# Branch weights in seven products, sums and lo parts on GpSimd, a wide third block: a change to a decoder layer on one core

## The chip, the core and the metric

The kernel runs on one core of one Trainium2 chip. The metric is the device time of one execution in microseconds (us). The names of the engines are those of the profile: PE is TensorE, DVE is VectorE, ACT is ScalarE, POOL is GpSimd, and SP is SyncE, which only issues DMAs here.

## The reference, cut to what matters

One decoder layer on x of 512 tokens by 1024, float32 throughout. Three token mixers are gated and added, then an output product, a feed-forward product with a gate, and two residuals:

```python
qa, ka, va, qb, kb, vb, qm, gl = split(rms_norm(x) @ w_in)
y_swa = swa_sink_attention(qa, ka, va, sinks, rel_bias)     # sliding window, 8 heads
y_sb  = stick_breaking_attention(qb, kb, vb)                # 8 heads
y_mem = memory_cross_attention(qm, mk, mv)                  # 4 heads, 256 memory rows
g = sigmoid(gl)                                             # 3 gates of 1024
merged = g[0] * (y_swa @ w_branch_swa) + g[1] * (y_sb @ w_branch_sb) + g[2] * (y_mem @ w_branch_mem)
h = x + rms_norm(merged @ w_out)
u = rms_norm(h)
out = h + rms_norm((silu(u @ w_gate) * (u @ w_up)) @ w_down)
```

Every product by y_ and w_branch_ is one of 512x512 by 512x1024. The weights w_gate and w_up have 2816 columns, 22 blocks of 128.

## The kernel before, in words

**Products in parts.** Each float32 operand is split in a hi part and a lo part (`split`, line 413: hi is rounded by ACT, lo = raw − hi is subtracted by DVE, from two SBUF operands). A product is hi·hi + hi·lo + lo·hi, three matmuls, each of 128 contracted rows and 256 or 512 columns.

**Seven products instead of eight.** Most of the large products are cut into two by two quarters and computed in the Strassen-Winograd way: seven products named p1 to p7 of sums of quarters, instead of eight. Sums of weight quarters are made by accumulating DMAs from POOL's queue, or by DVE; sums of the left operands by DVE. For the branch products, the ones in the list SEVENS (line 31) are made in sevens (`add_sevens`, `seven_*`), which are the sliding-window branch SWA and the memory branch MEM. The stick-breaking branch SB is made in eight by `add_branch`. `w_sum` (line 871) makes the weight sums of a branch in DRAM by two DMAs each on POOL's queue, started from unit SUM_FROM = 17 of the first half on. `seven_out` (line 907) multiplies a branch's result with its gate and adds the other branches; `gated` and `q_end` (lines 800 and 817) multiply the SB result with its gate as soon as the gate is there.

**Order of the first half.** After the projections come the heads (stick-breaking first), the three branches' gates, and the branch products. `sb_head` leaves z in three banks; ACT makes sigmoid(−z) and sigmoid(z) of it, POOL multiplies the blocks on the diagonal with the causal mask `seen` (lines 1272 to 1276: two operations of 128x128 and one of 128x2x128 for each head), DVE runs a scan along the keys, and PE transposes the result. Then come merging, w_out (loaded raw by `out_load`, split by `out_split`, line 1479), the norm, and the sums of the rows.

**Gate and up.** `gu` (line 1749) makes the block n (0 to 10) of w_gate and w_up together, in seven products for each n. A "banked" block (`banked`, line 1685) is wide: the moving operand holds the hi and the lo columns side by side, so hi·hi and hi·lo are one matmul of 512 columns, and only lo·hi is one of 256. Others take three matmuls of 256. Blocks 0 and 1 are narrow; from n = 3 on all are wide; in block 2 the banks y and w are wide and bank x, to which p1, p6, p7 and p4 go, is narrow. A wide block leaves two halves in PSUM, which `g_end` has to add: ACT copies one (t), then the other (t2, line 1711), and DVE adds them. `act_out` writes the activated quarters aq. After every second block `g_end` makes the sums of quarters sq, sr and aq(1,0) for the down product on DVE (line 1744).

**Down.** The products run in the order p1, p5, p6, p3, p7, p2, p4, each in six pieces c of up to 1024 weight columns (12 matmuls for the two halves of the tokens; `down`). For each piece ACT and DVE split the weights in hi and lo, in four buffers for each (hi0 to hi3, lo0 to lo3), and the left operands are split a few pieces ahead by `left_of` (line 1793) into lh and ll, tiles that rotate through a common ring. w_down arrives as raw for p1; p5 is made by an accumulating DMA of POOL's onto the same tile, after DVE has split p1's piece from it. p4 and p7 are made in the same way later, on POOL's queue. `dn_sum` adds two raw tiles on DVE for p6.

**What sets the order.** Each engine runs its instructions in its program's order. A table ORDER (from line 38 on) gives that order for each of the five engines by instruction numbers, and a table PLAN (from line 139 on) gives the place in the pools that each tile takes. Both are written out in the kernel. An instruction waits for its operands and for its tile's place, and all behind it on that engine wait with it.

Of the kernel before, what the change touches and what calls it, by code (L numbers as in the profile page):

```python
# [17 lines left out]
P = 128  # L18
# [12 lines left out]
SEVENS = (SWA, MEM,)  # L31
SUM_FROM = 17
# [25 lines left out]
    ),  # L58
    "vector": (
# [34 lines left out]
    ),  # L94
    "scalar": (
# [274 lines left out]
def tile_kernel(ctx, tc, a):  # L370
# [690 lines left out]
    for b in (SB, SWA, MEM):  # L1061
# [36 lines left out]
        if b in SEVENS:  # L1098
            add_sevens(b)
        elif b != SB:  # L1100
            add_branch(b)
# [1066 lines left out]
```

## Time and profile before

| What | us |
|---|---|
| median of 3 runs | 774.6 |
| lowest and highest | 774.45, 774.68 |
| the profiled execution | 774.24 |
| its span, first to last instruction | 772.4 |
| PE busy in it | 763.8 |
| DVE busy | 661.8 |
| ACT busy | 506.2 |
| POOL busy | 116.1 |

A row of the profile names the line of the instruction, its engine, its operation, what it writes and reads (out<-in), and its form. Every operation has line L222, since a helper records them, so tiles tell them apart: `bank` is PSUM, `lo<-raw,hi` the lo part of a weight tile, `bw` the stick-breaking weights of a head. In a timeline, the first column is the start and the second the duration, in us from the start of the span; neighbouring operations of one form are put together as xcount. An operation starts before its neighbour has ended where the engine overlaps them. A bracket gives the idle time ahead and what ended it.

### The profile page before, as it was taken

Reading aid. Unit: us, or ns where it says so; the run is one execution under the profiler, and the core shown is the slowest. Engines: PE = TensorE matmul, PEld = TensorE weight load, DVE = VectorE, ACT = ScalarE, POOL = GpSimd, SP = SyncE. Lnnn points to the kernel's source line nnn. Section 1 sums busy time; section 2 is a strip of 40 time slices with the busy share of each in tenths; the row PEclk is TensorE's granted clock in tenths of the full one; section 3 lists DMA queues with packets and bytes.
Section 4 is the critical chain, followed back from the end, with each engine's and each line's share of the span. In section 5 each row is a group of like instructions: output and inputs, shape, how many; then the busy total and the mean of one; then the engine's idle time right before and its main releaser. Section 6 shows DMA issues by size and latency. Waiting matters only on the chain.

```text
span 772.4 us, 11540 instructions
## 1 busy us (share of the span) xinstructions
PE 763.8 (99%) x4118; PEld 650.5 (84%) x4118; DVE 661.8 (86%) x1053; ACT 506.2 (66%) x916; POOL 116.1 (15%) x153
## 2 busy tenths in 40 slices
PE   9999999999999999999999999999999999999996
PEld 6889887778878888878888899988888888888885
DVE  7994797886796757999997589989999999999866
ACT  7662676796495758788935486566666668766552
POOL 3003363212002120011012001000000000214000
PEclk9999999999999999999999999999999999999999
DMA  8448998447239795579989338977777654959702
GB/s 304 145 132 245 340 253 251 138 130 157 56 82 189 194 195 185 136 188 247 390 200 294 101 93 238 251 209 181 205 192 207 179 157 150 204 136 242 168 1 109
DMA packets 48377, 144.28 MB, mean 187 GB/s; under 512 B 5760, under 2 KB 7344, under 8 KB 48256
## 3 DMA queue, kind: packets, MB, share of 16 engines
q1 hardware_dynamic: 33216, 92.55, 35.2%
q0 software_dynamic: 14672, 50.61, 33.6%
q8 instruction: 32, 0.52, 0.3%
q10 hardware_dynamic: 432, 0.39, 0.2%
q14 instruction: 25, 0.20, 0.1%
HBM read 134.61 MB, written 15.21 MB: 194 GB/s over the span
## 4 chain that ended last, share of the span: by engine, by line
PE 94%; DVE 2%; POOL 1%; ACT 1%; issue 1%; DVEq 0%; POOLq 0%; ACTq 0%
PE bank L222 94%; DVE bw L222 1%; POOL bw L222 0%; DVE lo L222 0%; POOL vnext L222 0%; POOL bias L222 0%; DVE wide L222 0%; ACT bw L222 0%; ACT L222 0%; ACT kas L222 0%; ACT br L222 0%; ACT hi L222 0%; DVE mks0l L222 0%; DVE fg L222 0%; ACT at L222 0%
## 5 line engine op out<-in xcount | busy, mean ns | idle before, releaser
L222 PE MATMUL bank<-pair,hi 128*128 128x512 f32 (+1 forms) x1064 | 263.2, 360 | 0.0
L222 PE MATMUL bank<-hi,pair 128*128 128x512 f32 (+1 forms) x696 | 215.8, 376 | 0.0
L222 PEld LDWEIGHTS bank<-pair,hi 128*128 128x128 f32 x1064 | 185.6, 189 | 26.6 <-issue 0.9
L222 DVE TENSOR_TENSOR lo<-raw,hi 128x1024 fp32r<-128x1024 f32 (+3 forms) x142 | 165.3, 1166 | 36.2 <-ACT hi L222 35.6
L222 ACT CAST hi<-raw 128x1024 fp32r<-128x1024 f32 (+3 forms) x142 | 143.3, 1012 | 79.2 <-PE bank L222 61.1
L222 PE MATMUL bank<-pair,lo 128*128 128x256 f32 (+1 forms) x776 | 166.3, 302 | 0.0
L222 PEld LDWEIGHTS bank<-hi,pair 128*128 128x128 f32 x696 | 128.1, 188 | 22.8 <-ACT mw L222 0.5
L222 PE MATMUL bank<-lo,pair 128*128 128x512 f32 (+1 forms) x362 | 136.0, 376 | 0.0
L222 PEld LDWEIGHTS bank<-pair,lo 128*128 128x128 f32 x776 | 122.0, 190 | 9.9
L222 ACT CAST hi<-wide 128x1024 fp32r<-128x1024 f32 (+1 forms) x62 | 63.2, 1024 | 35.9 <-PE bank L222 17.9
L222 PEld LDWEIGHTS bank<-lo,pair 128*128 128x128 f32 x362 | 68.0, 188 | 11.1
L222 DVE TENSOR_TENSOR lo<-wide,hi 128x1024 fp32r<-128x1024 f32 (+1 forms) x62 | 73.1, 1184 | 2.5 <-ACT hi L222 2.2
L222 POOL DMA_DIRECT2D raw<-in_w_g x24 | 21.0, 873 | 150.1 <-DVE lo L222 116.7
L222 DVE TENSOR_TENSOR gp<-gp,bank 128x512 f32<-128x512 f32 x48 | 32.9, 685 | 3.6 <-PE bank L222 2.7
L222 DVE TENSOR_TENSOR_SCAN bw<-br,bw 128x384 f32<-128x384 f32 (+3 forms) x32 | 29.1, 960 | 7.4 <-POOL bw L222 7.3
L222 POOL DMA_DIRECT2D raw<-in_w_gu x14 | 12.6, 943 | 128.8 <-DMA raw<-in_w_gu 128.6
L222 ACT ACTIVATE sg<-gp 128x256 f32<-128x256 f32 x41 | 17.3, 421 | 18.6 <-DVE gp L222 18.4
L222 POOL DMA_DIRECT2D wide<-in_w_gu x13 | 11.3, 873 | 106.4 <-DMA wide<-in_w_gu 90.8
L222 ACT COPY gp<-bank 128x512 f32<-128x512 f32 x41 | 23.9, 584 | 2.6 <-PE bank L222 2.6
L222 POOL TENSOR_TENSOR bw<-bw,wide 128x128 f32<-128x128 f32 (+1 forms) x24 | 18.6, 795 | 40.1 <-ACT bw L222 35.9
L222 DVE TENSOR_TENSOR gp<-gp,hp 128x512 f32<-128x512 f32 x33 | 22.5, 683 | 0.0
L222 DVE SCALAR_TENSOR_TENSOR s<-s,s 128x1 f32<-128x1 f32 x36 | 6.4, 177 | 17.6 <-ACT mt L222 10.5
(582 smaller groups left out, 1300.0 us busy)
## 6 DMA issues: line engine op xcount, KB each, us to landing
wide<-in_w_gu SPq DMA_DIRECT2D x30, 512.0 KB, 5.3
raw<-in_w_gu SPq DMA_DIRECT2D x27, 512.0 KB, 5.0
raw<-in_w_g POOLq DMA_DIRECT2D x24, 512.0 KB, 5.8
raw<-in_w_g SPq DMA_DIRECT2D x18, 512.0 KB, 3.8
raw<-in_w_p SPq DMA_DIRECT2D x14, 512.0 KB, 5.2
raw<-in_w_gu POOLq DMA_DIRECT2D x14, 512.0 KB, 7.6
wide<-in_w_gu POOLq DMA_DIRECT2D x13, 512.0 KB, 6.9
raw<-in_w_brt SPq DMA_DIRECT2D x10, 512.0 KB, 4.8
```

Source lines behind the costliest of these rows:

```text
L222: ins = f(*args, **kw)
```

## The change

- SB joins SEVENS: its branch product goes in seven quarter products, with `add_sevens(SB)` where `add_branch(SB)` stood. The weight sums start from unit 13 instead of 17, and there is one more branch of them: eight more DMAs on POOL's queue.
- The SB gate products (8 of 128x512) and the SWA adds in `seven_out` (8) go from DVE to POOL.
- The lo parts of w_out (16) go to POOL, and so do the lo parts of the left operands of the down product in pieces 0 to 4 (35), and the sums sq, sr and aq(1,0) of the column pairs 0 to 4 (15).
- The third mask operation of a stick-breaking head becomes two of 128x128.
- Bank x of gate and up block 2 is wide as well.
- ORDER and PLAN are drawn anew for all engines.

```diff
-SEVENS = (SWA, MEM,)
-SUM_FROM = 17
+SEVENS = (SB, SWA, MEM)
+SUM_FROM = 13
...
 ORDER = {
...
-        "1-2 0 98 3-15 20 17 16 18 21-23 19 24-27 41 28 42 29 43 30-32 47 44 38 35 33-34 45 48 53 49-52 46 36 54 59 55 "
+        "1-2 98 0 3-15 20 17 16 18 21-23 19 24-27 41 28 42 29 43 30-32 47 44 38 35 33-34 45 48 53 49-52 46 36 54 59 55 "
...
-    def split(raw, hi, lo):
+    def split(raw, hi, lo, eng=None):
...
-        lows = nc.vector.tensor_tensor(lo, raw, hi.bitcast(F32), op=ALU.subtract)
+        lows = (eng or nc.vector).tensor_tensor(lo, raw, hi.bitcast(F32), op=ALU.subtract)
...
-    def parts(name, t):
+    def parts(name, t, eng=None):
         h, l = ck(f"{name}h", F32R), ck(f"{name}l", F32R)
-        split(t[:, :], h[:, :], l[:, :])
+        split(t[:, :], h[:, :], l[:, :], eng)
...
             acc = acc_t[(t, h)]
-            nc.vector.tensor_tensor(acc[:, :], acc[:, :], x[:, :], op=ALU.mult)
+            nc.gpsimd.tensor_tensor(acc[:, :], acc[:, :], x[:, :], op=ALU.mult)
...
                 acc = acc_t[(2 + i, 0)]
-                nc.vector.tensor_tensor(acc[:, :], acc[:, :], t[:, :], op=ALU.mult)
+                nc.gpsimd.tensor_tensor(acc[:, :], acc[:, :], t[:, :], op=ALU.mult)
...
-        nc.vector.tensor_tensor(g[:, :], g[:, :], more[:, :], op=ALU.add)
+        (nc.gpsimd if b == SWA else nc.vector).tensor_tensor(g[:, :], g[:, :], more[:, :], op=ALU.add)
...
-    add_branch(SB)
+    add_sevens(SB)
...
-        if b in SEVENS:
+        if b != SB:
             add_sevens(b)
-        elif b != SB:
-            add_branch(b)
...
-            if i < 2:
-                nc.gpsimd.tensor_tensor(w[i][:, :P], w[i][:, :P], seen[:, :], op=ALU.mult)
-            else:
-                x = w[i][:, :].rearrange("p (b n) -> p b n", b=4)[:, 0:4:2, :]
-                nc.gpsimd.tensor_tensor(x, x, seen[:, :].unsqueeze(1).to_broadcast([P, 2, P]), op=ALU.mult)
+            for o in (0,) if i < 2 else (0, 256):
+                x = w[i][:, o : o + P]
+                nc.gpsimd.tensor_tensor(x, x, seen[:, :], op=ALU.mult)
...
-            wo[(h, k)] = parts(f"wo{h}{k}", t)
+            wo[(h, k)] = parts(f"wo{h}{k}", t, nc.gpsimd)
...
-        return n >= 2 and (n, b) != (2, "x")
+        return n >= 2
...
-            sub(sq[c], aq[(1, 0)][c], aq[(1, 1)][c], w)
-            sub(aq[(1, 0)][c], aq[(0, 0)][c], aq[(1, 0)][c], w)
+            eng = nc.gpsimd if n < HF - 1 else None
+            sub(sq[c], aq[(1, 0)][c], aq[(1, 1)][c], w, eng=eng)
+            sub(aq[(1, 0)][c], aq[(0, 0)][c], aq[(1, 0)][c], w, eng=eng)
             if n < HF - 1:
-                sub(sr[c], sq[c], aq[(0, 0)][c], w)
+                sub(sr[c], sq[c], aq[(0, 0)][c], w, eng=eng)
...
-    def sub(out, x, y, n, op=ALU.subtract):
-        nc.vector.tensor_tensor(out[:, :n], x[:, :n], y[:, :n], op=op)
+    def sub(out, x, y, n, op=ALU.subtract, eng=None):
+        (eng or nc.vector).tensor_tensor(out[:, :n], x[:, :n], y[:, :n], op=op)
...
-        split(x[:, :n], h[:, :n], l[:, :n])
+        split(x[:, :n], h[:, :n], l[:, :n], nc.gpsimd if c < NCH - 1 else None)
```

On POOL, at the start of the down phase, the rows before are DMAs alone. Those to `raw` and `wide` from in_w_dn accumulate into weight tiles of p5 (the first six rows) and of p4:

```order
L222 DMA raw_73<-in_w_dn 128x1024
L222 DMA wide_84<-in_w_dn 128x1024 x3
L222 DMA raw_74<-in_w_dn 128x1024
L222 DMA wide_84<-in_w_dn 128x512
L222 DMA raw_73<-in_w_dn 128x1024
L222 DMA wide_84<-in_w_dn 128x1024 x3
L222 DMA raw_74<-in_w_dn 128x1024
```

In the changed program the last DMAs of p5 stand in the same place, and operations of 128x512 between and behind them. Here `pair` and `ll` are lo tiles of the left operands, in the ring, and sq, sr and aq are sums of quarters:

```order
L230 DMA raw_73<-in_w_dn 128x1024
L230 TENSOR_TENSOR sq_5338<-aq_5084,aq_5110 128x512
L230 TENSOR_TENSOR aq_5084<-aq_5134,aq_5084 128x512
L230 DMA raw_75<-in_w_dn 128x1024
L230 DMA wide_84<-in_w_dn 128x512
L230 TENSOR_TENSOR ll_6338<-sq_5338,pair_109 128x512
L230 TENSOR_TENSOR sq_6047<-aq_5794,aq_5820 128x512
L230 TENSOR_TENSOR aq_5794<-aq_5844,aq_5794 128x512
L230 TENSOR_TENSOR pair_115<-aq_5084,pair_113 128x512
```

After the row of pair_115 fifteen more operations of 128x512 follow without a DMA between them, and then p4's first DMA. From p5's first DMA, which waits for DVE's split of p1's first piece, to p7's first one on a whole raw tile of p3 (it waits for the split of p3's first piece) there are 25 such operations.

On DVE, just behind the split of p1's second piece (`lo_81<-wide_84,hi_78`), the rows before hold lo parts of the left operands (`pair<-sq,lh`, `pair<-sq,pair`) between the splits of weights:

```order
L222 TENSOR_TENSOR lo_82<-wide_84,hi_76 128x1024
L222 TENSOR_TENSOR aq_6163<-gp_6032,sg_6161 128x256
L222 TENSOR_TENSOR pair_116<-sq_4944,lh_6279 128x512
L222 TENSOR_TENSOR pair_118<-aq_6163,pair_106 128x256
L222 TENSOR_TENSOR pair_111<-sq_5299,pair_115 128x512
L222 TENSOR_TENSOR pair_107<-sq_5654,pair_113 128x512
L222 TENSOR_TENSOR lo_83<-raw_74,hi_79 128x1024
```

In the changed program the splits there have the last column pair's work of 128x256 between them:

```order
L230 TENSOR_TENSOR lo_82<-raw_73,hi_76 128x1024
L230 TENSOR_TENSOR aq_6201<-gp_6071,sg_6199 128x256
L230 TENSOR_TENSOR gp_6225<-gp_6225,hp_6227 128x512
L230 TENSOR_TENSOR ll_6394<-sq_6234,pair_116 128x256
L230 TENSOR_TENSOR pair_106<-aq_6201,pair_111 128x256
L230 TENSOR_TENSOR sr_6341<-sq_6234,aq_6201 128x256
L230 TENSOR_TENSOR aq_6147<-aq_6201,aq_6147 128x256
L230 TENSOR_TENSOR lo_83<-raw_75,hi_79 128x1024
```

The three rows of 128x512 from sq are on POOL now. On PE, in gate and up block 2, the products of bank x took three matmuls of 256 columns for each k (two by hi, one by lo):

```order
L222 MATMUL bank_104<-pair_114,hi_78 128x256 x2
L222 MATMUL bank_104<-pair_114,lo_81 128x256
L222 MATMUL bank_104<-pair_106,hi_78 128x256 x2
L222 MATMUL bank_104<-pair_106,lo_81 128x256
L222 MATMUL bank_104<-pair_107,hi_77 128x512 x2
```

In the changed program they take one of 512 and one of 256:

```order
L230 MATMUL bank_104<-pair_111,hi_78 128x512 x2
L230 MATMUL bank_104<-pair_114,hi_78 128x512 x2
L230 MATMUL bank_104<-pair_111,lo_81 128x256 x2
L230 MATMUL bank_104<-pair_114,lo_81 128x256 x2
```

Over the program there are 64 matmuls of 256 columns fewer for that, and 32 of 512 more; the stick-breaking product has 12 of 512 fewer.

More of the change, by code (lines that the diff above doesn't have):

```diff
@@ L96 @@
         "0-16 21-22 18 17 19 23-25 20 26-29 38-39 30 40 31 43 32-33 41-42 34-35 46 36 44-45 37 49 47-48 52 50-51 55 53 "
[28 rows of a table removed]
[28 rows of a table added]
     ),
     "gpsimd": (
-        "4-11 15 31-32 3 0-1 13 12 14 2 39 41 53 55 40 42 54 56 16 21 46 26 29 28 30 60 33-35 20 18-19 17 22 24 23 "
-        "36-37 27 25 47 61 38 43-45 48 62 50-52 49 63 57-59 64-71 73 79 76 72 78 75 74 77 80-106 109 108 107 110-134 "
-        "143-148 139 135-138 140-142"
[8 rows of a table added]
     ),
     "sync": (
[5 rows of a table removed]
[5 rows of a table added]
     ),
@@ L140 @@
     "raw": (
-        "3 2 1 0 3 2 1 0 3 2 1 0 3 2 1 0 3 2 1 0 3 2 1 0 3 2 1 0 3 2 1 0 3 2 1 0 3 2 1 2 1 2 1 0 3 0 3 0 3 2 0 1 3 2 0 "
-        "1 3 2 3 2 3 2 0 3 1 2 0"
+        "0 1 2 3 0 1 2 3 0 1 2 3 0 1 2 3 0 1 2 3 0 1 2 3 0 1 2 3 0 1 2 3 0 1 2 3 0 1 2 3 0 1 0 1 0 1 2 3 2 3 2 3 0 1 2 "
+        "3 0 1 2 3 0 3 0 3 0 1 2 3 0 1"
     ),
     "hi": (
-        "3 2 1 0 3 2 1 0 3 2 1 0 3 2 1 0 3 2 1 0 3 2 1 0 3 2 1 0 3 2 1 0 3 2 1 0 2 3 1 0 2 3 1 0 2 3 1 0 2 3 1 0 2 3 1 "
-        "0 2 3 1 0 2 3 1 0 2 3 1 0 2 3 1 0 2 3 1 0 2 3 1 0 2 3 1 0 2 3 1 0 2 3 1"
+        "0 1 2 3 0 1 2 3 0 1 2 3 0 1 2 3 0 1 2 3 0 1 2 3 0 1 2 3 0 1 2 3 0 1 2 3 0 1 2 3 0 1 2 3 0 1 2 3 0 1 2 3 0 1 2 "
+        "3 0 1 2 3 0 1 2 3 0 1 2 3 0 1 2 3 0 1 2 3 0 1 2 3 0 1 2 3 0 1 2 3 0 1 2 3 0 1"
     ),
     "lo": (
-        "3 2 1 0 3 1 2 0 3 1 2 0 3 1 2 0 3 1 2 0 3 1 2 0 3 1 2 0 3 1 2 0 3 1 0 2 1 3 0 2 1 3 0 2 1 3 0 2 1 3 0 2 1 3 0 "
-        "2 1 3 0 2 1 3 0 2 1 3 0 2 1 3 0 2 1 3 0 2 1 3 0 2 1 3 0 2 1 3 0 2 1 3 0"
+        "0 1 2 3 0 1 2 3 0 1 2 3 0 1 2 3 0 1 2 3 0 1 2 3 0 1 2 3 0 1 2 3 0 1 2 3 0 1 2 3 0 1 2 3 0 1 2 3 0 1 2 3 0 1 2 "
+        "3 0 1 2 3 0 1 2 3 0 1 2 3 0 1 2 3 0 1 2 3 0 1 2 3 0 1 2 3 0 1 2 3 0 1 2 3 0 1"
     ),
     "p": (
[4 rows of a table removed]
[4 rows of a table added]
     ),
     "p2": (
-        "3 1 0 3 2 3 1 2 1 3 0 2 1 3 0 1 1 3 0 0 2 1 1 0 3 3"
+        "1 2 3 2 0 1 0 1 1 2 3 0 1 3 3 3 0 0 1 2 2 0 2 2 3 0 1"
     ),
     "ck": (
[19 rows of a table removed]
[20 rows of a table added]
     ),
     "ck2": (
-        "13 10 2 0 7 8 11 12 3 4 9 1 5 6"
+        "13 8 2 11 12 7 0 10 3 5 6 9 1 4"
     ),
@@ L193 @@
     "fraw": (
-        "8 1 3 2 0 7 6 5 4 8 1 3 2 0 7 8 4 5 2 6 3 7 1 0 8 5 6 4 2 3 1 8 0 7 5 4 3 2 6 1 0 5 7 8 4 2 1 3 6 0 7 4 8 5 2 "
-        "3 0 1 6 7 8 2 5 4 3 0"
+        "8 2 3 0 1 6 7 4 5 8 2 3 0 1 6 8 5 4 0 3 7 6 2 1 8 4 3 0 5 7 2 8 6 1 4 0 7 3 5 2 6 4 8 1 0 3 2 7 5 6 8 0 1 4 3 "
+        "7 6 5 2 8 1 3 4 0 7 6"
     ),
```

223 rows, old and new, of tables (ORDER, PLAN) are left out of this document.

## Prediction

> **What bounds the kernel now.** I read the page first: the busy shares, the slices, and the chain that ended last.
>
> ```profile
> PE 763.8 (99%) x4118; PEld 650.5 (84%) x4118; DVE 661.8 (86%) x1053; ACT 506.2 (66%) x916; POOL 116.1 (15%) x153
> PE   9999999999999999999999999999999999999996
> DVE  7994797886796757999997589989999999999866
> PE 94%; DVE 2%; POOL 1%; ACT 1%; issue 1%; DVEq 0%; POOLq 0%; ACTq 0%
> ```
>
> TensorE (PE) is busy in 99% of the span, in every slice but the last, and 94% of the last chain is its own. VectorE (DVE) stands at 9 in long runs of slices; GpSimd (POOL) is nearly empty. So time can be won only by taking matmul work away, and it is lost wherever another engine hands PE its operands late. How close the others are, the table of busy time by stage tells (window; length; PE; PEld; DVE; ACT; POOL; clock; DMA share; GB/s):
>
> ```profile
> 330.00:395.00 65.00, 65.00 (x300) 53.25 (x299) 64.61 (x96) 54.12 (x89) 6.99 (x8) 1.00 0.95 275
> 395.00:460.00 65.00, 65.00 (x376) 57.05 (x375) 49.73 (x106) 32.92 (x88) 6.48 (x8) 1.00 0.60 163
> 650.00:700.00 50.00, 50.00 (x236) 41.93 (x236) 49.63 (x71) 38.71 (x62) 10.79 (x13) 1.00 0.79 190
> 700.00:740.00 40.00, 40.00 (x178) 33.14 (x177) 35.49 (x58) 25.18 (x46) 6.76 (x8) 1.00 0.73 168
> ```
>
> PE is full in all of them, and DVE is full beside it in 330 to 395 (memory branch) and in 650 to 700 (the start of the down projection). The granted clock is 1.00 and plays no part. There DVE is the second bound, and there a change that makes DVE slower will show.
>
> **PE's gain.** PE's pace is the distance of neighbouring starts; the second column is longer because matmuls overlap.
>
> ```profile
> 439.65 0.39 PE L222 MATMUL bank<-wo15l,mgh 128*128 128x512 f32 x1
> 439.88 0.39 PE L222 MATMUL bank<-pair,mgl 128*128 128x512 f32 x1
> 440.11 0.39 PE L222 MATMUL bank<-wo16h,mgh 128*128 128x512 f32 x1
> 300.03 0.28 PE L222 MATMUL bank<-pair,qms0h 128*128 128x256 f32 x1
> 300.26 0.28 PE L222 MATMUL bank<-pair,pair 128*128 128x256 f32 x1
> ```
>
> A matmul of 512 columns takes 0.23 us (0.2275 over longer stretches), one of 256 takes (300.26 − 300.03) / 2, or 0.12. The stick-breaking branch product goes from eight quarter products to seven: 96 matmuls of 512 columns become 84, so 12 × 0.2275 = 2.73 us. In the third gate and up block, bank x goes wide: 96 matmuls of 256 become 32 of 512 and 32 of 256, so 64 × 0.12 − 32 × 0.2275 = 0.40. Together **−3.13 us**, all on the path, since PE is the path. That is all there is to win, beside the few waits that PE has.
>
> **What the move to GpSimd costs DVE.** By the program 82 two-input operations of 128x512 go onto POOL, most of them from DVE, which is relieved by about 37 us in all. The price is read where both engines already work at once: POOL's masks for the stick-breaking weights, and DVE's scans beside them (start; duration).
>
> ```profile
> 85.63 0.96 DVE L222 TENSOR_TENSOR_SCAN bw<-br,bw 128x384 f32<-128x384 f32 x1 [1.95 <-POOL bw L222]
> 86.81 0.73 POOL L222 TENSOR_TENSOR bw<-bw,wide 128x256 f32<-128x256 f32 x1
> 95.29 1.65 POOL L222 TENSOR_TENSOR bw<-bw,wide 128x256 f32<-128x256 f32 x1
> 96.33 1.42 DVE L222 TENSOR_TENSOR_SCAN bw<-br,bw 128x384 f32<-128x384 f32 x1
> 116.17 1.42 DVE L222 TENSOR_TENSOR_SCAN bw<-br,bw 128x384 f32<-128x384 f32 x1
> 85.14 0.46 POOL L222 TENSOR_TENSOR bw<-bw,wide 128x128 f32<-128x128 f32 x1 [0.66 <-ACT bw L222]
> 113.89 0.95 DVE L222 TENSOR_TENSOR mks0l<-mk,pair 128x512 fp32r<-128x512 f32 x1
> 94.36 0.69 DVE L222 SCALAR_TENSOR_TENSOR qa<-bank,wide 128x512 f32<-128x512 f32 x1 [0.80 <-PE bank L222]
> ```
>
> A scan of 128x384 takes 0.96 us when its POOL partner is small or done, and 1.42 when a 128x256 one is in its way: DVE lost 0.46 to 0.50 against an operation of 0.73. The POOL operation itself went from 0.73 to 1.65, that is by the length of a scan. So the two don't share, they take turns. Against a 128x128 one (0.46 alone) DVE's mks0l took 0.95, where other operations of its size take 0.68: 0.27 lost. Only DVE operations with both inputs in SBUF pay; qa, which reads a PSUM bank, kept its 0.69 with a POOL mask beside it.
>
> From 0.27 at 128 elements and 0.50 at 256 the line goes on to 0.50 + 2 × 0.23, about **0.95 us lost by DVE per POOL operation of 512** (an estimate from these rows; no operation of that size stands on POOL before). In the same way POOL's own time goes from 0.46 and 0.73 to about 1.28 alone, and to 1.28 plus one DVE operation when DVE is full. What DVE saves per moved operation is its pace (starts of neighbours):
>
> ```profile
> 654.23 1.22 DVE L222 TENSOR_TENSOR lo<-raw,hi 128x1024 fp32r<-128x1024 f32 x1
> 655.37 0.68 DVE L222 TENSOR_TENSOR pair<-aq,pair 128x512 fp32r<-128x512 f32 x1
> 655.97 1.40 DVE L222 TENSOR_TENSOR gp<-gp,bank 128x512 f32<-128x512 f32 x2
> 660.75 0.42 DVE L222 TENSOR_TENSOR aq<-gp,sg 128x256 f32<-128x256 f32 x1
> 661.09 0.68 DVE L222 TENSOR_TENSOR pair<-sq,lh 128x512 fp32r<-128x512 f32 x1
> ```
>
> 1.14 us for 1024 elements, 0.60 for 512, 0.34 for 256. So 0.60 is freed and up to 0.95 comes back as waiting: where DVE has time to spare this costs nothing, where it is full each move is a loss.
>
> The Trainium skill, "SBUF — State Buffer", section "Who interferes with whom", says that a DVE instruction with two SBUF inputs contends with a GpSimd one that reads SBUF, and that the loser blocks for the whole instruction. The turns in the rows agree with it; the size doesn't quite, for DVE lost 0.50 of 0.73, two thirds. With the whole 1.28 as the price, the sum below would end 7.6 us higher.
>
> **The down phase.** The program order puts a dense run of POOL work between the raw split of p1's first piece and that of p3's first, the stretch in which DVE was full before. These two splits, and PE's first matmuls on them:
>
> ```profile
> 701.08 1.22 DVE L222 TENSOR_TENSOR lo<-wide,hi 128x1024 fp32r<-128x1024 f32 x1
> 661.22 0.40 PE L222 MATMUL bank<-lo,pair 128*128 128x512 f32 x1
> 706.12 0.39 PE L222 MATMUL bank<-lo,pair 128*128 128x512 f32 x1
> 666.63 0.69 DVE L222 TENSOR_TENSOR lo<-wide,hi 128x512 fp32r<-128x512 f32 x1
> 674.84 0.39 PE L222 MATMUL bank<-lo,pair 128*128 128x512 f32 x1
> ```
>
> PE takes 706.12 − 661.22 = 44.9 us from one to the other. The first split was done at 655.45, 5.8 ahead of PE; the second at 702.30, 3.8 ahead. The greatest lead here was 7.5 (split done at 667.32, used at 674.84); the four lo buffers, freed by PE one unit of 2.73 us after the other, don't allow more than about 8. By the program DVE has 65 instructions between the two splits before (18 of 1024, 36 of 512, 11 of 256: 20.5 + 21.6 + 3.7 = 45.8 us, and the trace has 46.9) and 50 after (18, 19, 13: **36.2 us**). POOL has 25 operations of 128x512 in between, among DMA issues that wait for just these splits. Five of DVE's 50 read PSUM, 8% of its time, so 23 of the 25 are charged: 23 × 0.95 = 21.9, and DVE needs 58.1. It has 44.9 plus the lead it enters with. I give it 7.5, the greatest of before, since it is relieved ahead of the stretch too: 52.4, so PE waits 5.7; with the 5.8 of before it would wait 7.4. I take **+5.6 us** (0 to 7.4). The waits fall on the splits of p6 and p3, and what PE loses there never comes back.
>
> **The memory branch.** Sixteen lo parts of w_out and eight gated adds of the sliding-window branch go to POOL around 340 to 400. The lo parts are wanted later, and DVE has 65 − 49.7 = 15.3 us free in 395 to 460, so I let them cost nothing. The adds lie in the full stretch: 8 × (0.95 − 0.60) = 2.8 at most, and some of DVE's work beside them evacuates PSUM: **+1.5 us** (0 to 2.8).
>
> **Edits at nothing.** POOL also gets eight gate products of the stick-breaking heads and the masks in pieces of 128 (16 × 0.27 = 4.3 us of DVE's time for 8 × 0.50 = 4.0). They lie in 75 to 170, where DVE has 18 us free; at most 8 × 0.35 or 2.8, if each hits a scan that PE waits for.
>
> ```profile
> 75.00:170.00 95.00, 94.21 (x552) 77.50 (x551) 77.18 (x118) 69.76 (x141) 34.68 (x47) 1.00 0.78 230
> L222 POOL DMA_DIRECT2D raw<-in_w_g x24 | 21.0, 873 | 150.1 <-DVE lo L222 116.7 <-DVE s L222 32.7 <-DVE wide L222 0.7
> ```
>
> The sums of the stick-breaking weights add eight DMAs to POOL's queue at 0.87 us each, some between the masks of the heads, where a mask may come late; POOL was busy 34.7 of 95 there, so nothing. ACT's added copies, about 13 us, lie in its idle third.
>
> **The sum.** 774.24 (the profiled execution; its span is 772.4, 1.8 lies around it) − 3.1 + 5.6 + 1.5 = 778.2. The median of the runs shown, 774.6, is 0.36 above the profiled one: **778.6 us**. A measurement of this kernel can tell about 0.2%, 1.5 us, from no change.
>
> **Rivals.**
>
> *Faster: the price isn't paid on the path.* Then PE's 3.1 us remain: 771.5, or up to 773 with some waits. For it: what moved is wanted late, DVE is relieved of 37 us, and the price is stretched from operations a quarter and half as long. The point from which it decides: with a price of p per operation PE waits 36.2 + 23p − 52.4; that is zero below p = 0.70, and eats all 3.1 us at p = 0.84. The 0.95 isn't far above either, so 0.36.
>
> *No change:* p near 0.84, or a lead that is spent elsewhere: 773.1 to 776.1, with 0.11.
>
> *Slower by POOL's queue instead of DVE.* p4's and p7's accumulating DMAs stand behind the same run of operations on POOL, and the last pieces of p7 had no slack in before:
>
> ```profile
> 687.88 0.89 POOL L222 DMA_DIRECT2D raw<-in_w_dn  x1 [18.75 <-DVE lo L222]
> 702.59 0.88 POOL L222 DMA_DIRECT2D wide<-in_w_dn  x1 [2.00 <-DVE lo L222]
> 725.18 1.22 DVE L222 TENSOR_TENSOR lo<-raw,hi 128x1024 fp32r<-128x1024 f32 x1
> 726.75 0.39 PE L222 MATMUL bank<-lo,pair 128*128 128x512 f32 x1
> ```
>
> PE used that lo part 0.35 us after it was there. If DVE wins the turns, POOL takes 1.28 + 0.60 for each of the 25, 47 us, and 7 issues of 0.87 make it 53: about 3 more than the 50 at hand between these two splits. p7 then comes 3 to 6 us late, and the time is 774.6 − 3.1 + 3 to 6, 774.5 to 777.5. Against it: the order has p7's first DMAs ahead of p4's last, which takes some of that back. It has 0.08, half of it within 0.2%.
>
> **Chances and range.** Slower 0.49 (0.45 by DVE's price, 0.04 by POOL's queue), same 0.15 (0.11 and 0.04), faster 0.36. The likeliest case has 776.2 to 784.5 for itself: the top is 774.6 − 3.1 + 7.4 + 2.8 + 2.8. Since the cases of the other side hold half, the range goes down to 771.0: 771.5, less half a microsecond of waits that a new order may take away.
>
> **What would show it.** In the trace after: PE's work smaller by 3.1; POOL rows of 128x512 of 1.3 us alone and near 1.9 beside DVE; DVE splits of 128x1024, 1.22 before, at 1.8 to 2.2 in many places of the down phase; PE's waits named DVE lo, at p6 and p3. Splits that keep 1.22 while POOL works beside them would make the price wrong. Long splits without a wait of PE would make the lead wrong. A wait on DMA ahead of p7 would be the third case.

## The result and the profile after

| What | before | after |
|---|---|---|
| median, us | 774.5 | 813.6 (4 runs, 813.2 to 817.2) |
| ratio after to before | | 1.0515, interval 1.0485 to 1.0545 |
| the profiled execution | 774.24 | 817.21 |
| its span | 772.4 | 815.4 |

The changed kernel is 39 us slower, and 43.0 in the profiled pair: the profiled execution is the slowest of the four, so what the trace shows is 3.6 us more than the median has. The side was right, the size was not: 778.6 was forecast, 784.5 at most.

From the page of after, the busy shares, PE's slices, the granted clock, and the last chain:

```profile
PE 780.3 (96%) x4074; PEld 654.8 (80%) x4074; DVE 697.9 (86%) x988; ACT 516.2 (63%) x941; POOL 268.6 (33%) x251
PE   9999999999999999989899999999999998869796
PEclk9999999999999999999999999999999998979898
PE 50%; DVE 17%; issue 5%; ACT 4%; DMA 1%; DVEq 0%; ACTq 0%
```

DVE has 65 instructions fewer and is busy 36 us longer; POOL's busy time has more than doubled. PE has fewer matmuls and a longer busy time, with a granted clock below full in the last slices. The chain that was 94% PE's is half PE's now. The table of busy time by stage, same columns as before:

```profile
330.00:395.00 65.00, 61.85 (x275) 50.01 (x273) 54.19 (x65) 48.85 (x78) 32.68 (x22) 0.97 0.74 197
395.00:460.00 65.00, 62.06 (x308) 51.76 (x309) 48.02 (x94) 28.96 (x78) 19.53 (x17) 0.97 0.77 208
650.00:700.00 50.00, 44.24 (x215) 37.14 (x214) 49.45 (x48) 35.88 (x60) 29.86 (x22) 0.93 0.62 137
700.00:740.00 40.00, 32.00 (x117) 24.51 (x117) 38.42 (x26) 16.12 (x24) 33.66 (x21) 0.87 0.26 59
```

In the last row DVE is busy for 38.4 of 40 us with 26 instructions, where it did 58 before. PE's waits follow (sum, times, longest). Of the tiles, `gp` and `sy` are those in which DVE adds up the banks of a product, and `mpts20l` is the lo part of an operand of the memory branch:

```profile
PE bank L230 <- DVE lo L230: 12.5, 7, 4.8
PE bank L230 <- DVE gp L230: 5.1, 2, 4.2
PE bank L230 <- DVE sy L230: 3.0, 1, 3.0
PE bank L230 <- DVE mpts20l L230: 2.3, 1, 2.3
PE bank L230 <- DVE wide L230: 2.0, 3, 1.3
PE bank L230 <- ACT hi L230: 1.9, 1, 1.9
```

**Where the time went.** For every matmul I take the distance to the next start, less the pace of its size (0.227 us for 512 columns, 0.12 for 256). The paces add up to 757.2 us before and 754.0 after: the saved work is there, 3.2. What lies above them, in us by stage:

| Stage | 0–170 | 170–300 | 300–340 | 340–460 | 460–650 | 650–700 | 700–end | sum |
|---|---|---|---|---|---|---|---|---|
| before | 4.4 | 0.1 | 0.9 | 0.6 | 1.1 | 0.0 | −0.2 | 7.0 |
| after | 4.4 | 3.4 | 1.8 | 10.4 | 3.2 | 9.2 | 20.9 | 53.3 |

46.3 more, less 3.2, is 43.1; the spans differ by 43.0. Of the 46.3, 31.6 are waits of over 0.18 us, and 11.7 are matmuls at half pace (95 of them, 31 before), which the prediction had no term for. They stand behind the longer waits. PE in the changed kernel, behind its wait for `gp`, and the same group of work before that wait:

```profile
669.11 2.00 PE L230 MATMUL bank<-pair,hi 128*128 128x512 f32 x8
...
676.22 3.78 PE L230 MATMUL bank<-pair,hi 128*128 128x512 f32 x8 [4.16 <-DVE gp L230]
679.80 1.90 PE L230 MATMUL bank<-pair,lo 128*128 128x256 f32 x8
```

Eight matmuls take 3.78 us instead of 2.00, and the eight of 256 columns behind them 1.90, where they took 1.11 at 670.95. So the wait of 4.2 us costs some 2.6 us more. In this kernel a single wait of 2.35 us is enough:

```profile
349.48 0.50 PE L230 MATMUL bank<-mpts20l,pair 128*128 128x512 f32 x1 [2.35 <-DVE mpts20l L230]
...
350.96 0.63 PE L230 MATMUL bank<-hi,xsp50h 128*128 128x512 f32 x1
351.38 0.63 PE L230 MATMUL bank<-lo,xsp50h 128*128 128x512 f32 x1
```

From 350.96 the starts are 0.42 apart. Behind a wait of 1.16 us (at 698.08) they stay 0.23 apart. No single length divides the two cases: in all_back (below) eight such matmuls stand behind a wait of 1.82 us at 395.75, and in sums_back none behind one of 3.41 at 755.20.

**What DVE and POOL do to each other.** Both engines' timelines of the changed kernel at 700 us, DVE's rows and then POOL's:

```profile
702.41 2.31 DVE L230 TENSOR_TENSOR lo<-wide,hi 128x1024 fp32r<-128x1024 f32 x1
704.64 4.55 DVE L230 TENSOR_TENSOR lo<-raw,hi 128x1024 fp32r<-128x1024 f32 x2
```

```profile
701.37 2.27 POOL L230 TENSOR_TENSOR sr<-sq,aq 128x512 f32<-128x512 f32 x1
703.60 2.28 POOL L230 TENSOR_TENSOR pair<-aq,pair 128x512 fp32r<-128x512 f32 x1
705.83 2.28 POOL L230 TENSOR_TENSOR ll<-sr,lh 128x512 fp32r<-128x512 f32 x1
```

They take turns, one for one: a split starts every 2.23 us, where its pace was 1.14, so each POOL operation costs DVE 1.1 us. Here the forecast's mechanism is to be seen, at 1.1 where it took 0.95. It is the SBUF reads that count: in this trace 28 two-input DVE operations of 128x512 that read a bank and overlap a POOL operation took 0.67 to 0.69 us, as alone; of those with both inputs in SBUF 31 overlap one, and their median is 1.76. What the forecast did not foresee is this DVE row, and POOL's beside it:

```profile
751.14 10.83 DVE L230 TENSOR_TENSOR lo<-raw,hi 128x1024 fp32r<-128x1024 f32 x1 [0.73 <-ACT hi L230]
```

```profile
748.90 2.67 POOL L230 DMA_DIRECT2D bp<-in_w_dn  x3 [0.86 <-DVE lo L230]
750.66 3.47 POOL L230 TENSOR_TENSOR pair<-aq,pair 128x512 fp32r<-128x512 f32 x2
753.15 1.82 POOL L230 DMA_DIRECT2D raw<-in_w_dn  x1
753.76 2.54 POOL L230 TENSOR_TENSOR pair<-aq,pair 128x512 fp32r<-128x512 f32 x1
755.02 2.51 POOL L230 TENSOR_TENSOR ll<-aq,lh 128x512 fp32r<-128x512 f32 x1
756.25 2.13 POOL L230 DMA_DIRECT2D wide<-in_w_dn  x1
756.86 2.81 POOL L230 TENSOR_TENSOR ll<-aq,lh 128x512 fp32r<-128x512 f32 x1
758.09 5.01 POOL L230 TENSOR_TENSOR ll<-aq,pair 128x512 fp32r<-128x512 f32 x2
```

Of its 10.8 us the split needs 1.1 for itself. It was held off while POOL ran six operations and the DMA issues between them, and the seventh ended behind it. PE waited 4.8 us for this split. In first_back and sums_back (below), the same split is held off too and takes 8.4 and 9.5 us. The Trainium skill, "SBUF — State Buffer", section "Who interferes with whom", says that issue order, not the operation's shape, decides who blocks. That fits; these rows show besides that one side can be held off over a whole run of instructions.

### The profile page after: what moved, and what is told of

It reads as the page before. It is cut to its first block, busy times and chain, and to the rows that moved or that the text cites. A ratio compares the mean times of both kernels' runs of the same rounds, so it can differ in the third digit from the quotient of the medians.

```text
span 815.4 us, 11531 instructions
## 1 busy us (share of the span) xinstructions
PE 780.3 (96%) x4074; PEld 654.8 (80%) x4074; DVE 697.9 (86%) x988; ACT 516.2 (63%) x941; POOL 268.6 (33%) x251
## 4 chain that ended last, share of the span: by engine, by line
PE 50%; DVE 17%; issue 5%; ACT 4%; DMA 1%; DVEq 0%; ACTq 0%
PE bank L230 50%; DVE lo L230 7%; DVE gp L230 3%; ACT hi L230 1%; DVE raw L230 1%; DVE wide L230 1%; DVE aq L230 1%; DMA wo<-in_w_out 1%; DVE sr L230 1%; ACT w L230 1%; DMA raw<-in_w_g 0%; ACT mw L230 0%; DVE gq2p L230 0%; DVE sy L230 0%; ACT L230 0%
## 5 line engine op out<-in xcount | busy, mean ns | idle before, releaser
L230 DVE TENSOR_TENSOR lo<-raw,hi 128x1024 fp32r<-128x1024 f32 (+3 forms) x148 | 200.4, 1358 | 39.2 <-ACT hi L230 38.4
L230 PE MATMUL bank<-hi,pair 128*128 128x512 f32 (+1 forms) x580 | 184.6, 381 | 3.8 <-DVE sy L230 3.0
L230 PE MATMUL bank<-lo,pair 128*128 128x512 f32 (+1 forms) x308 | 118.1, 384 | 11.3 <-DVE lo L230 11.3
L230 PEld LDWEIGHTS bank<-hi,pair 128*128 128x128 f32 x580 | 109.1, 192 | 24.6 <-DVE sy L230 3.5
L230 PEld LDWEIGHTS bank<-lo,pair 128*128 128x128 f32 x308 | 59.4, 193 | 22.9 <-DVE lo L230 13.4
L230 POOL TENSOR_TENSOR bw<-bw,wide 128x128 f32<-128x128 f32 x32 | 24.8, 794 | 23.5 <-ACT bw L230 23.5
L230 DVE TENSOR_TENSOR_SCAN bw<-br,bw 128x512 f32<-128x512 f32 (+3 forms) x32 | 28.0, 917 | 4.8 <-POOL bw L230 4.6
L230 DVE TENSOR_TENSOR gp<-gp,hp 128x512 f32<-128x512 f32 x36 | 30.9, 858 | 0.0
L230 PE MATMUL bank<-hi,ll 128*128 128x512 f32 x70 | 28.4, 406 | 0.0
L230 POOL DMA_DIRECT2D xq<-xq x8 | 7.0, 891 | 58.2 <-DVE lo L230 39.3
```

The source lines that it names most:

```text
L230: ins = f(*args, **kw)
```

## The experiments

The kernel before is at 774.6 to 775.1 us in them.

**Operations back on DVE.** `all_back` puts all 82 operations of 128x512 onto DVE. The rest, the orders too, is as changed; each goes to the place in DVE's order where it had run on POOL. `left_back` does so with the 35 lo parts of the left operands, `sums_back` with the 15 sums, `first_back` with the other 32.

```diff
+MOVE = {100: 330, 99: 332, 105: 375, 104: 345, 107: 349, 108: 348, 110: 350, 111: 351, 118: 386, 119: 403, 123: 446,
...
+            g = getattr(self.other, name) if self.other is not None and len(self.seen) in MOVE else f
+            ins = g(*args, **kw)
...
+        self.gpsimd.other = nc.vector
...
+                if e == "vector":
+                    seq += [nc.gpsimd.seen[m] for m, behind_k in MOVE.items() if behind_k == k]
```

> The changed kernel with all 82 operations of 128x512 back on VectorE, each put into VectorE's order where GpSimd ran it in the trace; sevens, wide block, DMAs and the rest of the orders as changed. Theory (the two engines take turns at SBUF, each GpSimd operation stops VectorE for about 1.1 us): the waits of TensorE and its slow matmuls after them go, and most of the 3.1 us of matmul work shows: 771 to 778 us. Rival 1 (the redrawn orders, the eight added DMAs or the seven products are late by themselves): 800 us or more. Rival 2 (VectorE can't carry this work in any case): TensorE still waits for lo parts, 785 to 800.

> The changed kernel with only the 35 lo parts of the down product's left operands back on VectorE. Theory: the waits from the end of gate and up to the end of the down phase go, which are some 21 us of waiting and some 9 us of slow matmuls behind them in the trace: 783 to 792 us. Rival 1 (orders and DMAs): within 5 us of the changed kernel, 808 to 814. Rival 2 (no room on VectorE): 795 to 808.

> The changed kernel with the 16 lo parts of w_out, the 8 gate products and the 8 adds back on VectorE. Theory: the waits between 300 and 410 us (some 7 us, and some 3 us of slow matmuls) go: 801 to 806 us. Rival 1: 810 to 815.

> The changed kernel with the 15 sums sq, sr and aq back on VectorE. Theory: five of them stand in the dense run of the down phase, ten in stretches where VectorE has time; 2 to 8 us go: 805 to 812 us. Rival 2 would have the same work cost more on VectorE: 814 to 820.

Measured: all_back 791.9 us (1.0222, 1.0205 to 1.0239); left_back 798.9 (1.0314, 1.0293 to 1.0335); first_back 810.7 (1.0466, 1.0445 to 1.0487); sums_back 810.9 (1.0468, 1.0439 to 1.0497). So the moves to POOL cost 21.7 us: 14.7 for the left lo parts, 2.7 for the sums, 2.9 for the rest, which add up to 20.3. The two small ones are no wider than the spread of the runs (sums_back has two, 809.0 and 812.8). But 17.3 us against before remain with nothing moved. So only sums_back is where the theory put it; all_back and left_back came out in the ranges of rival 2, no room on VectorE, and first_back in that of rival 1. Rival 2 is answered below, by an order in which DVE carries all of it in 777.7 us. PE's waits in all_back:

```profile
PE bank L241 <- DVE lo L241: 3.1, 2, 2.3
PE bank L241 <- DVE wide L241: 2.7, 3, 1.3
PE bank L241 <- DVE gp L241: 1.9, 1, 1.9
PE bank L241 <- DVE sy L241: 1.8, 1, 1.8
PE bank L241 <- ACT gq2p L241: 1.1, 1, 1.1
```

They lie at 170 to 230, 337 to 410, and from 668 on: many small ones, for operations that come late from DVE and ACT. Each of the 82 operations stands where POOL had run it, and that need not be a good place in DVE's order, so the 17.3 us are the loss of the drawn order and of these places together.

**The price by itself.** Three kernels are made from before. `left_moved` moves only the 35 left lo parts to POOL. `idle_adds` puts 16 adds of 128x192 on POOL at 669 us, on a tile of their own that nothing reads. `idle_sets` puts 16 memsets there instead.

```diff
+    scr = base.tile([P, 192], F32, name="scr")
...
+    idle_work = [nc.gpsimd.tensor_tensor(scr[:, :], scr[:, :], scr[:, :], op=ALU.add) for _ in range(16)]
...
+                if e == "gpsimd" and k == 134:
+                    seq += idle_work
```

> The kernel before with one part of the change: the 35 lo parts of the down product's left operands on GpSimd, each put into GpSimd's order where VectorE ran it; orders otherwise as before, no sevens for the stick-breaking branch, block 2 as before. Theory: VectorE saves 35 x 0.6 = 21 us of work and is stopped for up to 35 x 1.1 = 38 us: TensorE waits 10 to 20 us in the down phase, with slow matmuls behind the longer waits: 784 to 800. Rival (the orders, not the place of the work, cost the time): 773 to 777.

> The kernel before, with 16 additions of 128x192 on GpSimd that read and write a tile of their own, which no other instruction uses, put where GpSimd idles in the down phase (668 to 688 us). Nobody waits for them but the DMAs behind them on GpSimd's queue. Theory (each stops VectorE's two-input operations, by about 0.4 us at this size): VectorE loses some 6 us there, more than TensorE's lead of 4: 777 to 780 us, and VectorE rows longer than before beside them. Rival (what costs is waiting for GpSimd's results, or its queue): within 1 us of 774.6, VectorE's rows as before.

> As the kernel with the idle additions, with 16 memsets of the same tile of 128x192 in their place, which write SBUF and read nothing. Theory (it is the reading of two SBUF operands on both engines that makes them take turns): 774 to 775 us, VectorE's rows as before. If any work on GpSimd slowed VectorE, 776 or more.

Measured: left_moved 802.0 us (1.0354, 1.0333 to 1.0374); idle_adds 778.4 (1.0051, 1.0036 to 1.0066); idle_sets 774.6 (1.0001, 0.9991 to 1.001). DVE beside the idle adds, and beside the memsets:

```profile
671.26 0.99 DVE L222 TENSOR_TENSOR pair<-sr,pair 128x512 fp32r<-128x512 f32 x1
672.17 1.52 DVE L222 TENSOR_TENSOR lo<-raw,hi 128x1024 fp32r<-128x1024 f32 x1
```

```profile
670.99 0.69 DVE L222 TENSOR_TENSOR pair<-sr,pair 128x512 fp32r<-128x512 f32 x1
671.59 1.22 DVE L222 TENSOR_TENSOR lo<-raw,hi 128x1024 fp32r<-128x1024 f32 x1
```

Each add of 192 elements costs the DVE operation beside it 0.30 us. A memset, which reads nothing, costs none. The memsets hold POOL for 5.4 us only and the adds for 18.3, but the DMA behind the adds is not late by POOL either: when they are done it waits 5.9 us more for DVE's split. So it is not POOL's queue that costs the time here. With the rows before, the price is 0.27 at 128 elements, 0.30 at 192, 0.50 at 256 and 1.1 at 512. The adds alone, without any use of their results, cost the program 3.9 us. The 35 lo parts cost 27.4 us in the old order, 0.78 each, 2 us above the top of what was expected. It is not the price of turns alone: PE's waits there name ACT with 11.9 us and DVE's `lo` with 6.0. Two of ACT's three waits hang on DVE operations that were held off and took 5.7 and 5.3 us; the last, of 5.4 us, hangs on POOL's own lo parts, for which ACT had waited 8.9.

**Who is held off.** `adds_behind_dma` has the 16 idle adds in four groups, each right behind one of p4's DMA issues.

```diff
-                if e == "gpsimd" and k == 134:
-                    seq += idle_work
+                if e == "gpsimd" and k in (143, 144, 145, 146):
+                    seq += idle_work[(k - 143) * 4 : (k - 142) * 4]
```

> The kernel before with the same 16 unconnected GpSimd adds of 128x192 as in the run with idle adds (778.4 us), only placed in four groups of four, each right behind one of the four accumulating p4 transfers that GpSimd issues. If a GpSimd run that stands behind a DMA issue gives the waiting vector operation no turn (as with the 8 to 11 us operation in the changed kernel): one vector operation beside each group takes 2.5 us or more (1.2 to 1.5 us by turns), four such rows, and PE waits of 1 us or more behind them. Rival (turns alternate there too, and the long rows came from something else): no vector row there above 1.6 us, about 0.3 us lost by each of some 16 operations, and a time of 775 to 779 us.

Measured: 788.3 us (1.0173, 1.0159 to 1.0187), +13.5. Neither expectation had it: not DVE was held off, but POOL. The add's tile (min/median/max duration), POOL's rows, DVE's where its turn ends, and PE's wait:

```profile
L222 POOL TENSOR_TENSOR scr<-scr x16: 568/836/12283, 689.3 to 716.9; 128x192 f32<-128x192 f32 x16
```

```profile
688.71 0.89 POOL L222 DMA_DIRECT2D raw<-in_w_dn  x1 [18.76 <-DVE lo L222]
689.27 15.29 POOL L222 TENSOR_TENSOR scr<-scr 128x192 f32<-128x192 f32 x4
704.50 0.87 POOL L222 DMA_DIRECT2D wide<-in_w_dn  x1
```

```profile
700.77 0.42 DVE L222 TENSOR_TENSOR aq<-aq,aq 128x256 f32<-128x256 f32 x1
701.29 0.81 DVE L222 TENSOR_TENSOR ll<-sr,pair 128x512 fp32r<-128x512 f32 x1
702.02 1.52 DVE L222 TENSOR_TENSOR lo<-wide,hi 128x1024 fp32r<-128x1024 f32 x1
```

```profile
PE bank L222 <- ACT hi L222: 10.0, 1, 10.0
```

One add waited 12.3 us while DVE ran seventeen operations without a gap. It ended where DVE paused for the first time: 700.77 + 0.42 is 701.19, and the next row starts at 701.29. From then on they take turns. p4's DMAs stood behind the add, their transfers came late, ACT had nothing to split, and PE waited 10 us. So either side can keep the other out, DVE here until its first pause, POOL above until its run was all but over; between two engines that both stay busy turns are not sure. What sets off the one or the other stays open: a DMA issue stands ahead of DVE's long split above, but also ahead of this add.

**The order.** The rest of the loss, the 17 us of all_back, may be the drawn order's (with the places of the 82 operations in it), or that of the load which the seven products put on DVE and ACT. Five kernels keep the changed arithmetic, PE's order and everything on DVE, and draw the orders of DVE and ACT anew (`redrawn`; from 160 us on, `redrawn_late`; from 300, `redrawn_later`; `redrawn_late` drawn once more, `redrawn_twice`; and `redrawn_late` up to 270 us with `redrawn_twice` behind, `redrawn_joined`). In all, the edit is that of all places, and new tables:

```diff
-            wo[(h, k)] = parts(f"wo{h}{k}", t, nc.gpsimd)
+            wo[(h, k)] = parts(f"wo{h}{k}", t)
...
-        split(x[:, :n], h[:, :n], l[:, :n], nc.gpsimd if c < NCH - 1 else None)
+        split(x[:, :n], h[:, :n], l[:, :n])
```

> The changed program with all 82 split, sum and product operations on the vector engine, as in the run with everything taken back (791.9 us), but with the orders of the vector and scalar engines drawn anew for that load; the seven quarter products, the wide third banks and TensorE's own order stay. Theory (the 17 us that were left are the order's: the changed orders put the left factors' and w_out's low parts where a vector engine without help cannot finish them): 771 to 775 us, PE's waits after 160 us under 4 us in sum (15.7 before this), half-pace matmuls back to about 31. Rival (with the sevens the vector engine's own load is what PE waits for, in any order): 785 us or more, with the same waits at 340 to 400 us and after 660 us.

> As the first redrawing, but vector and scalar engine keep the changed kernel's order up to 160 us, and each operation that splits a loaded weight is placed no earlier than its transfer landed in the run with everything taken back. The first redrawing lost 6 us in the first 60 us and 10 us of waits from 337 to 437 us, where scalar-engine splits stood ahead of late transfers, and none after 440 us. Theory (order, not the load that the sevens give): 773 to 777 us, PE waits after 160 us under 4 us in sum, none above 1 us. Rival (the load of vector and scalar engine at 330 to 440 us, with the sevens' sums, w_out's splits and the residual, is too much for any order): 780 us or more, with waits over 6 us in sum between 330 and 440 us.

> As the redrawing from 160 us on, but vector and scalar engine keep the changed kernel's order up to 300 us. What the order costs between 170 and 300 us (3.2 us more than the kernel before in the run with everything taken back) stays; so the theory that the order is the cause gives 3 us more than the redrawing from 160 us on, 776 to 780 us, and the rival the same 780 us or more with waits at 330 to 440 us.

> As the redrawing from 160 us on (784.8 us), drawn once more from that run's own landing times, with two splits of loaded gate and up weights that stood on the scalar engine ahead of the second gate block's evacuations (its 4.4 us wait at 422 us and the half-pace matmuls behind it) put behind them, and the order kept only up to 100 us. Theory (order): the wait at 422 us goes, 777 to 781 us, and half-pace matmuls back to about 31. Rival (load): another wait of 3 us or more takes its place between 340 and 460 us, and the time stays at 783 us or more.

> Joined from two redrawn orders: vector and scalar engine follow the redrawing from 160 us on (784.8 us) up to 270 us and the second redrawing (779.1 us) behind that. The second one is 2.9 us later at PE's 1500th matmul (287.5 against 284.6 us) and has hardly a wait after 311 us. Theory (all that is left is the order's): 775 to 777.5 us; what then still stands against the kernel before lies ahead of 320 us. Rival (the second redrawing has only moved its loss, the load comes back as waits behind 320 us): 779 us or more.

Measured: redrawn 798.1 us (1.03, 1.0286 to 1.0314), worse than all_back; redrawn_late 784.8 (1.0138, 1.012 to 1.0155); redrawn_later 787.0 (1.0158, 1.0143 to 1.0173); redrawn_twice 779.1 (1.0053, 1.0039 to 1.0066); redrawn_joined 777.7 (1.0036, 1.0022 to 1.005). By their numbers the first three speak for the load, redrawn_twice for the order, and redrawn_joined lies between its two ranges. But the traces show few places: redrawn is 6 us late at PE's 250th matmul already (62.9 against 57.0 us in all_back), has PE waiting from 337 to 440 us, and behind that no wait above 0.22. The longest, in ACT's timeline of redrawn and in PE's waits:

```profile
431.21 0.19 ACT L228 ACTIVATION_READ_ACCUMULATOR mt<-bank 128x1 f32 x1
434.97 1.04 ACT L228 CAST hi<-wide 128x1024 fp32r<-128x1024 f32 x1 [3.58 <-DMA wide<-in_w_gu]
```

```profile
PE bank L228 <- ACT mgh L228: 6.3, 1, 6.3
PE bank L228 <- ACT hi L228: 4.2, 2, 3.7
```

A split stands ahead of `mgh`, the evacuation of the next merged block, and waits for its transfer; all behind it on ACT waits too, PE in the end. In redrawn_late the same splits still cost a wait of 4.2 us there; redrawn_twice has them behind the evacuations, and that wait is gone. The stage that was worst in the changed kernel, in redrawn_joined:

```profile
650.00:700.00 50.00, 50.00 (x241) 42.14 (x240) 50.00 (x72) 40.81 (x65) 6.16 (x7) 1.00 0.68 161
700.00:740.00 40.00, 39.86 (x175) 32.32 (x174) 34.75 (x56) 22.49 (x38) 11.52 (x13) 1.00 0.94 209
```

PE is full again, at full clock. The table of above for these kernels:

| Stage | 0–170 | 170–300 | 300–340 | 340–460 | 460–650 | 650–700 | 700–end | sum |
|---|---|---|---|---|---|---|---|---|
| all_back | 4.7 | 3.4 | 2.2 | 8.7 | 1.6 | 2.4 | 6.1 | 29.0 |
| redrawn_joined | 4.2 | 2.1 | 1.7 | 2.4 | 1.7 | 0.0 | 0.6 | 12.9 |

The orders of DVE and ACT alone, the places of the 82 operations among them, are worth 16.1 of the 22.0 us that all_back has more than before in the traces (14 by the medians). 5.9 are left in the best order that I found, 4.6 of them from 170 to 460, where the seven products' sums and evacuations lie. Whether a still better order takes them, or they are the load's, stays open. They are more than the 3.2 that the change saves on PE, so no version here beats the kernel before.

## Why the prediction was right on the side and wrong on the size

The forecast missed by 35.0 us, 813.6 less 778.6. With nothing moved, all_back stands 17.3 us above before where the sum had 3.1 below it: that is 20.4 of them. The moves cost 21.7 where the sum had 5.6 + 1.5: that is the other 14.6. So two steps failed: the redrawn orders, which the sum took at nothing, and the down phase, which it bounded at 7.4. The division holds for this way of taking the change apart; in the old order the 35 lo parts alone cost 27.4. The side doesn't hang on the failed steps: either loss is larger than PE's gain.

- **PE's gain, −3.13:** right; 757.2 to 754.0.
- **The price, 0.95 per operation:** mechanism right (both sides in SBUF, turns, POOL stretched by DVE's length), size 1.1. A POOL operation beside a split of 1024 takes 2.28, as 1.28 plus a turn of nearly 1 would.
- **The down phase, +5.6, at most 7.4:** the mis-sized term. From 650 us on after has 30.1 us above the paces, all_back 8.5, before none. So 21.6 are the moves', four times the term. The price is not what failed: with 1.1 the same sum gives 36.2 + 23 × 1.1 − 52.4, or 9.1. The step that failed is the bound: DVE's load in one stretch against one lead. The loss has more parts: half-pace matmuls behind waits (8.0 us from 650 on), a held-off split (4.8 us of wait) in a later run of POOL operations that was left out of the sum, and a wait of 4.2 us for `gp` ahead of the down product. The waits do fall on `lo`, as the forecast said, but not on them alone.
- **The memory branch, +1.5 (0 to 2.8):** for the moved operations nearly right as far as the runs can tell, since taking all 32 early ones back gains 2.9. But the stage from 340 to 460 lost 9.8 us, of which 8.1 stay in all_back.
- **What the sum did not have:** the drawn orders themselves. It gave no reason for that: it took the new order as if it kept PE as well fed as the old one, and speaks of it only as taking away half a microsecond of waits. With all operations back on DVE, this order is worse than a new one by 14 us of time (791.9 to 777.7), the places of the 82 operations included. The rest of the 20.4, some 6 us, stays open between order and load.
- **The front and the masks, nothing:** right; 4.4 and 4.4 up to 170 us. The 3.3 us lost from 170 to 300 are in all_back too, so they are not the moves'; no term of the sum had them.
- **The rival of POOL's queue:** not what slowed the changed kernel, whose waits name DVE; but adds_behind_dma shows that it exists, by a held-off add, at 13.5 us.
- **The rival "faster", 0.36:** it needed a price under 0.84 and hung on the lead alone; with 1.1 it was out. PE's 3.1 us didn't remain even with nothing moved: the best order found stands 2.6 us above before.

## What to carry to other kernels

Where DVE is full, an operation on two SBUF tiles of 128x512 that goes to GpSimd takes more of DVE's time than it frees (0.60 freed, 1.1 lost here): move what reads nothing from SBUF, as the memsets do, or put it beside DVE work that reads PSUM, which kept its 0.68. A redrawn order is a change of its own: time it with the moved work put back, before the move is judged. And price a wait of TensorE with the slow matmuls behind it.

## What was not expected of the hardware

- TensorE at half pace, 0.42 us instead of 0.23, for 8 to 15 matmuls behind single waits of 2.35 us and more in the changed kernel, not behind one of 1.2: 11.7 us there. Between these, other kernels of the case have it behind a wait of 1.82, and not behind one of 3.41. The Trainium skill, "TensorE: Matmul & The Clock Gate", section "HAM oscillation — how this bites in real kernels", warns of gaps over about 3.4 us; here shorter ones suffice.
- The turns of DVE and GpSimd can fail to come: 10.8 us for a DVE split of 1.1, 12.3 for a GpSimd add of 0.57.
- A GpSimd memset costs DVE nothing, 0.69 and 1.22 beside it as without.
